# A two-layer decoder trunk on one core: other banks for one score span, and two changes of order on the engines

## Chip, core and metric

The kernel runs on one core of one Trainium2 chip. The metric is the device time of one execution in microseconds (us), given as the median of several runs; lower is better. A core has several engines that work side by side, each through a stream of instructions of its own: TensorE (PE) multiplies matrices and writes its results into eight PSUM banks, ScalarE (ACT) and VectorE (DVE) work on the elements of tiles, GpSimd (POOL) does a few small things here, and SyncE (SP) issues most of the transfers from memory.

## What is computed

The input is 512 tokens of 1024 numbers. Each of the two layers is a mixer and then a feed-forward network (FFN), each with a root-mean-square norm ahead of it and behind it and a residual sum. Cut to what matters here:

```python
for i in range(2):
    h = even_mixer(rms_norm(x, pre_g)) if i == 0 else odd_mixer(rms_norm(x, pre_g))
    x = x + rms_norm(h, post_g)
    h = conv_ffn(rms_norm(x, ffn_pre_g[i]), ...)      # (silu(gate) * up) @ w_down
    x = x + rms_norm(h, ffn_post_g[i])

def stick_breaking_attention(q, k, v):                # part of odd_mixer
    z = q @ k.T * scale
    log_beta = log_sigmoid(z)
    log_keep = where(strict, log_sigmoid(-z), 0)
    after = cumsum(log_keep, reverse=True) - log_keep
    return where(strict, exp(log_beta + after), 0) @ v
```

## The kernel before, in words

**Stages.** The program goes once through first mixer, first FFN, second mixer, second FFN, for all 512 tokens. Tokens are cut into four tiles of 128, taken in the order 3, 2, 1, 0 (`ORDER`). Every fp32 product is made from three products of halves (`mm3`, L263 to L265): each operand is split into a high part (ACT copies it, L72 or L171) and a low part (DVE subtracts, L73 or L172).

**Columns.** The next stage needs the normed tokens as columns. For a tile i, `mean_square` squares and sums X[i] on ACT (L188) and POOL makes the factor (L178, L181); `normed` multiplies on DVE in two halves (L546 in the first FFN, L1284 in the second mixer); `turned` gives back a function that, when called, transposes eight blocks on PE (L211) into two banks and splits each bank into xh (ACT, L171) and xl (DVE, L172). "Columns" below means this function.

**Sums.** `part_of` multiplies half of a tile's output by the gain on DVE (L225) and squares it on ACT (L230), and the residual is added on DVE (L542, L1308) once POOL has the factor (L180, L181).

**Banks.** The eight banks are rings by tag: "a" has three, "s" two, "t", "o" and "n" one each. A tile that takes a bank waits until the one that last had it has been read.

**Order.** In most stages a scheduler orders each engine's stream. At the end of the first FFN (from L530) and at the second mixer's end (from L1289) a `manual_schedule` keeps PE, DVE, ACT and POOL in the order in which the program is written; only the splits of weights are put in between. Weights come by DMA into three raw buffers, are split ahead of time into five pairs of buffers, and a pair is free again when PE has used it.

**Place 1: stick-breaking scores** (`sb_scores`, from L1047). For each of two pairs of heads, scores stand in three spans of 512, 384 and 384 columns; the third holds two blocks, of 256 and 128 columns. Each span takes two banks, one for each head y, and the two heads' products use two halves of PE's rows. PE makes the scores (L1057), DVE adds the mask to each block (L1061), and later instructions make the weights; in between PE makes four projections (`proj_T`, banks of ring "a", tile apt). Spans 1 and 3 both take the two banks of ring "s".

**Place 2: the second mixer's end** (loop from L1290). For each tile n: 12 products into the first half's bank, then the square of the tile before (X[j]), then the first half's product and square, then the columns of the tile before that one (`turns.pop(0)()`), then 12 products of the second half. The last two tiles' columns are called from inside the second FFN's first products (at k of 2 and 6), which read tiles 3 and 2 first (tile u, L263 to L265).

**Place 3: the first FFN's last sum** (from L553). `bank_done("c", 1)` makes the last 12 products (4 terms of 3) into a bank that `part_of` reads afterwards; columns of tile 3 stand ahead of it. The products of the second mixer (tile av) follow.

Of the kernel before, what the change touches and what calls it, by code (L numbers as in the profile page):

```python
# [86 lines left out]
def trunk(tc, A, out):  # L87
# [3 lines left out]
    with ExitStack() as top:  # L91
# [15 lines left out]
        def bank(tag, name, *shape):  # L107

            t = pp.tile([P, S], F32, tag=tag, name=name, bufs=BANKS[tag])
            if not shape:  # L110
                return t[:]
            n = math.prod(shape)
            names = "abc"[:len(shape)]
            return t[:, :n].rearrange(f"p ({' '.join(names)}) -> p {' '.join(names)}",
                                      **dict(zip(names, shape)))
# [89 lines left out]
        def turned(i, xnT, tags, xn):  # L205

            def turn():
                for n, k0 in enumerate((0, 4)):
                    tp = bank(tags[n], "tp", 4, P)
                    for k in range(4):  # L210
                        PE.transpose(tp[:, k], xn[:, (k0 + k) * P:(k0 + k + 1) * P], ident[:])  # L211
                    d = (slice(None), slice(k0, k0 + 4), slice(i * P, (i + 1) * P))
                    split(xnT[0][d], xnT[1][d], tp)

            return turn

        def part_of(t, ms, n, a, g, between=None, dve_first=False):

            c = slice(n * S, n * S + S)
            o = t[:, c]  # L220
            if isinstance(a, tuple):
                DVE.tensor_tensor(o, *a, ALU.subtract)  # L222
                a = o
            def product():
                DVE.tensor_tensor(o, a, g[:, c], ALU.mult)  # L225

            if dve_first:
                product()
            junk = chp.tile([P, D], BF16, tag="junk", name="junk", bufs=1)
            ACT.activation(junk[:, :S], a, AF.Square, scale=D ** -0.5, accum_out=ms[:, n:n + 1])  # L230
            if between:
                between()
            if not dve_first:
                product()

        def begin(pool=None, tag="s"):
            return ((pool or chp).tile([P, D], F32, tag=tag, name="t", **({"bufs": 2} if tag in ("z", "sp") else {})),
                    begin_sum())
# [22 lines left out]
        def mm3(o, lh, ll, rh, rl, first, last, more=False):  # L261

            PE.matmul(o, lh, rh, start=first, stop=False, skip_group_check=more)  # L263
            PE.matmul(o, lh, rl, start=False, stop=False, skip_group_check=more)  # L264
            PE.matmul(o, ll, rh, start=False, stop=last, skip_group_check=more)  # L265
# [17 lines left out]
        def row_product(acc, terms, first, last, halves=(0, 1)):  # L283

            for half in halves:
                c = slice(half * S, half * S + S)
                for n, (lh, ll, wh, wl) in enumerate(terms):
                    mm3(acc[half], lh, ll, wh[:, c], wl[:, c], first and n == 0, last and n == len(terms) - 1)
# [57 lines left out]
        def ffn(layer, xnT, pending, final):  # L346
            with ExitStack() as es:
# [15 lines left out]
                for half in (1, 0):  # L363
                    t = slice(half * 2 * P, (half + 1) * 2 * P)
# [32 lines left out]
                for n, f in enumerate(PAIRED):  # L397
# [4 lines left out]
                    for z in range(2):  # L402
# [8 lines left out]
                        c = cw[:, f, z]  # L411
# [33 lines left out]
                def product(m, s, g, at, w, half, first, last, more=False):  # L445
                    t = slice(at * P, (at + 1) * P)
                    c = slice(half * S, half * S + S)
                    mm3(bk[m, s], g[0][:, t], g[1][:, t], w[0][:, c], w[1][:, c], first, last, more)
# [34 lines left out]
                def later_product(m, s, n, ws):  # L483
                    at, w, half = PLAN[m]
                    product(m, s, later[n], at(s), ws[w], half, False, n == HF - 1, True)
# [24 lines left out]
                ws = [[W.next(), W.next()] for _ in range(TAIL)]  # L510
                nx = None if final else new_xnT()

                def bank_done(m, s):
                    for n in range(TAIL):
                        later_product(m, s, HF - TAIL + n, ws[n])
                    return bk[m, s]

                if final:

                    with tc.manual_schedule(engines={DVE.engine, ACT.engine, POOL.engine}):  # L520
                        for s in range(2):
                            i, j = 3 - 2 * s, 2 - 2 * s
                            t, ms = begin()
# [20 lines left out]
                def normed(i, r, t):  # L544
                    for c in (slice(0, S), slice(S, D)):
                        DVE.scalar_tensor_tensor(t[:, c], X[i][:, c], r[:, 0:1], g_next[:, c], ALU.mult, ALU.mult)  # L546

                def turn(i, t):
                    return turned(i, nx, "tn", t)

                (t2q, m2), (t0, m0) = early_q
                t3, m3 = begin()
# [14 lines left out]
                q2 = mean_square(X[2][:])  # L567
                b1 = bank_done("b", 1)
                DVE.tensor_tensor(t1[:, S:], uu[:, 1], b1, ALU.subtract)
                turn(3, t3)()  # L570
                part_of(t1, m1, 1, t1[:, S:], g_post, lambda: normed(2, q2, t2q))
                r1 = rstd(m1[:, 0:1], m1[:, 1:2])
                c1 = bank_done("c", 1)
                W.ahead(W.pos + 4)
                add_to(1, t1, r1)
                q1 = []
# [1 line left out]
                def last():  # L578
# [5 lines left out]
                turns = [(4, turn(2, t2q), lambda: (q1.append(mean_square(X[1][:])), last())),  # L584
                         (5, turn(1, t1), lambda: q1.append(mean_square(X[0][:]))),
                         (6, lambda: normed(0, q1[1], t0), turn(0, t0))]
# [370 lines left out]
        def odd(xnT, pending, order):  # L957
            xh, xl = xnT
            with ExitStack() as es:
# [56 lines left out]
                for i in ORDER:  # L1016
                    t = slice(i * P, (i + 1) * P)
                    a = bank("a", "av12")
                    at, *parts = pending.pop(0) if pending else (KD, )
                    for k in range(KD):  # L1020
# [4 lines left out]
                        c = slice((k % 2) * 512, (k % 2 + 1) * 512)  # L1025
# [23 lines left out]
                def sb_scores(u):  # L1049

                    zs = [sb.tile([P, 1280], F32, tag="z", name="z", bufs=2) for _ in range(2)]
                    for n, (j0, o0, o1) in enumerate(spans):
                        zp = [bank(t, "zp") for t in ("ss", "nt", "ss")[n]]
                        for j in (j0,) if j0 < 2 else (2, 3):
                            for y in range(2):
                                r = slice(y * 64, y * 64 + 64)
                                PE.matmul(zp[y][:, off[j] - o0:off[j + 1] - o0], sk[u][r, j * P:(j + 1) * P],  # L1057
                                          sq[u][r, j * P:], start=True, stop=True)
                        for y in range(2):
                            for j in (j0,) if j0 < 2 else (2, 3):  # L1060
                                DVE.tensor_tensor(zs[y][:, off[j]:off[j + 1]], zp[y][:, off[j] - o0:off[j + 1] - o0],  # L1061
                                                  smask[:, :S - j * P], ALU.add)

                    sps = []
                    for z in zs:
                        sp = sb.tile([P, 1280], F32, tag="sp", name="sp", bufs=2)
                        DVE.tensor_scalar(sp[:], z[:], 40.0, None, ALU.min)
                        ACT.activation(sp[:], sp[:], AF.Exp)
                        sps.append(sp)
                    return list(zip(zs, sps))  # L1070
# [217 lines left out]
                norms, turns = [], []  # L1288
                with tc.manual_schedule(engines={PE.engine, DVE.engine, ACT.engine, POOL.engine}):  # L1289
                    for n, i in enumerate(ORDER):  # L1290
                        q = slice(i * P, (i + 1) * P)
                        acc = [bank("as"[i % 2], "ao") for _ in range(2)]
                        terms = [(oS[0][:, k, q], oS[1][:, k, q], *wout[2 + k]) for k in range(2)]
                        terms += [(oG[0][k][:, q], oG[1][k][:, q], *wout[k]) for k in range(2)]
                        t, ms = begin(sb, ("z", "sp")[n % 2])
                        row_product(acc, terms, True, True, (0,))
                        if n:
                            j, tj = norms.pop()
                            rj = mean_square(X[j][:])
                        part_of(t, ms, 0, acc[0], g_post, dve_first=True)  # L1300
                        if n > 1:
                            turns.pop(0)()
                        row_product(acc, terms, True, True, (1,))
                        if n:
                            normed(j, rj, tj)
                        part_of(t, ms, 1, acc[1], g_post)
                        r = rstd(ms[:, 0:1], ms[:, 1:2])
                        DVE.scalar_tensor_tensor(X[i][:], t[:], r[:, 0:1], X[i][:], ALU.mult, ALU.add)  # L1308
                        norms.append((i, t))
                        turns.append(turned(i, nx, "na", t))  # L1310

                    r = mean_square(X[i][:])
# [6 lines left out]

        xnT = even()  # L1320
        xnT = ffn(0, *xnT, False)
        xnT = odd(*xnT)
        ffn(1, *xnT, True)


# [97 lines left out]
```

## Time and profile before

| | us |
|---|---|
| median of 3 runs (1162.73 to 1166.18) | 1164.73 |
| the profiled execution's own time | 1163.55 |
| its span, first to last instruction | 1161.8 |
| PE busy in it | 1143.3 |
| DVE busy | 810.8 |
| ACT busy | 557.9 |

A page of the profile describes one execution. PE's multiplications are pipelined, so the row of one lasts longer than the distance to the next: the distance of two starts says what one costs. In a timeline, a row gives start, duration, engine, line, operation, tiles (out<-in), shape and count, and in brackets the idle time ahead of it and what ended it.

### The profile page before, as it was taken

To read this page: it belongs to the slowest core of one execution; us is meant where nothing else is said; L and a number is where in the kernel's file an instruction comes from. 1 tells how busy PE (TensorE), PEld (TensorE's weight loads), DVE (VectorE), ACT (ScalarE), POOL (GpSimd) and SP (SyncE) were. 2 spreads that over 40 slices of the span, in tenths; PEclk is the share of its full clock that TensorE was granted. 3 is DMA by queue.
4 is the path that set the end of the run, shared out by engine and by line. 5 is a ranking of instruction groups with operands and counts; after the bars stand their busy time and mean duration, and the time that the engine had idled before them with its cause. 6 is when DMAs were issued, how large, how long until landed. Compare 5 with 4: busy or idle time off the path is not lost. (4 is left out here: it accounts for less than half of the span.)

```text
span 1161.8 us, 15175 instructions
## 1 busy us (share of the span) xinstructions
PE 1143.3 (98%) x5656; PEld 940.0 (81%) x5656; DVE 810.8 (70%) x1424; ACT 557.9 (48%) x942; POOL 57.0 (5%) x138
## 2 busy tenths in 40 slices
PE   8999999999999999999999999999999999999997
PEld 7876667898888888888888877898988888888885
DVE  6677676467766766899874465577676666679895
ACT  5565555245434434456543454545443443445562
POOL 2100012110000000000030000002000000000001
PEclk9999999999999999999999999999999999999999
DMA  7310521034333332355826213222233333324461
GB/s 278 121 64 1 170 73 37 37 130 128 93 104 93 94 105 84 100 156 162 251 93 177 73 55 93 92 73 94 91 109 96 104 91 97 103 82 145 145 200 73
DMA packets 39049, 126.81 MB, mean 109 GB/s; under 512 B 4672, under 2 KB 6336, under 8 KB 38848
## 3 DMA queue, kind: packets, MB, share of 16 engines
q1 hardware_dynamic: 37056, 122.11, 33.5%
q10 hardware_dynamic: 1920, 3.74, 1.1%
q8 instruction: 44, 0.72, 0.3%
q14 instruction: 29, 0.24, 0.1%
HBM read 117.95 MB, written 6.29 MB: 107 GB/s over the span
## 5 line engine op out<-in xcount | busy, mean ns | idle before, releaser
L73 DVE TENSOR_TENSOR wl<-wraw,wh 128x1024 fp32r<-128x1024 f32 (+1 forms) x202 | 244.4, 1218 | 181.1 <-ACT wh L72 180.9
L72 ACT CAST wh<-wraw 128x1024 fp32r<-128x1024 f32 (+1 forms) x202 | 209.5, 1046 | 282.8 <-PE u L264 179.4
L263 PE MATMUL u<-xh,wh 128*128 128x512 f32 (+1 forms) x768 | 285.0, 372 | 0.9 <-ACT xh L171 0.9
L264 PE MATMUL u<-xl,wh 128*128 128x512 f32 (+1 forms) x768 | 285.2, 372 | 0.1
L265 PE MATMUL u<-xh,wl 128*128 128x512 f32 (+1 forms) x768 | 285.1, 371 | 0.0
L263 PEld LDWEIGHTS u<-xh,wh 128*128 128x128 f32 x768 | 144.5, 188 | 26.3 <-ACT xh L171 1.3
L264 PEld LDWEIGHTS u<-xl,wh 128*128 128x128 f32 x768 | 144.7, 188 | 25.1 <-DVE xl L172 0.3
L265 PEld LDWEIGHTS u<-xh,wl 128*128 128x128 f32 x768 | 144.7, 188 | 24.8
L265 PE MATMUL acc<-wh,gl 128*128 128x512 f32 x248 | 96.5, 389 | 0.0
L264 PE MATMUL acc<-wl,gh 128*128 128x512 f32 x248 | 96.5, 389 | 0.0
L263 PE MATMUL acc<-wh,gh 128*128 128x512 f32 x248 | 96.4, 390 | 0.0
L417 ACT ACTIVATE y<-y 128x512 f32<-128x512 f32 x44 | 27.7, 632 | 85.1 <-DVE y L415 85.1
L412 ACT ACTIVATE y<-u,cw 128x512 f32<-128x512 f32 x88 | 67.4, 773 | 1.7 <-PE u L265 1.7
L415 DVE SCALAR_TENSOR_TENSOR y<-u,cw,y 128x510 f32<-128x510 f32 x88 | 65.6, 747 | 2.5
L413 DVE SCALAR_TENSOR_TENSOR y<-u,cw,y 128x511 f32<-128x511 f32 x88 | 65.1, 743 | 0.9 <-ACT y L412 0.9
L178 POOL TENSOR_TENSOR rv<-ms,epst 128x1 f32<-128x1 f32 x40 | 10.5, 263 | 913.7 <-ACT junk L230 841.4
L263 PEld LDWEIGHTS acc<-wh,gh 128*128 128x128 f32 x248 | 46.6, 188 | 10.2 <-issue 0.6
L265 PEld LDWEIGHTS acc<-wh,gl 128*128 128x128 f32 x248 | 46.6, 188 | 9.8
L264 PEld LDWEIGHTS acc<-wl,gh 128*128 128x128 f32 x248 | 46.6, 188 | 9.5
L263 PE MATMUL apt<-xh,wh 128*128 128x512 f32 x128 | 50.6, 395 | 0.0
L264 PE MATMUL apt<-xl,wh 128*128 128x512 f32 x128 | 50.0, 391 | 0.0
L265 PE MATMUL apt<-xh,wl 128*128 128x512 f32 x128 | 49.9, 390 | 0.0
(298 smaller groups left out, 1905.7 us busy)
## 6 DMA issues: line engine op xcount, KB each, us to landing
wraw<-in_ffn_w_up SPq DMA_DIRECT2D x88, 512.0 KB, 3.6
wraw<-in_ffn_w_down SPq DMA_DIRECT2D x44, 512.0 KB, 3.7
wraw<-in_od_w_dqk SPq DMA_DIRECT2D x12, 512.0 KB, 3.7
wraw<-in_ffn_w_down SPq DMA_DIRECT2D x22, 256.0 KB, 2.7
wraw<-in_ev_w_dqk SPq DMA_DIRECT2D x8, 512.0 KB, 4.0
wraw<-in_ev_w_out SPq DMA_DIRECT2D x8, 512.0 KB, 3.6
spill<-X SPq DMA_DIRECT2D x8, 512.0 KB, 2.6
X<-spill SPq DMA_DIRECT2D x8, 512.0 KB, 6.3
```

What stands on the lines that cost most here:

```text
L72: self.nc.scalar.copy(h[:, :w], raw[:, :w])
L73: self.nc.vector.tensor_tensor(l[:, :w], raw[:, :w], h[:, :w].bitcast(F32), ALU.subtract)
L178: POOL.tensor_tensor(v[:, :n], ms, epst[:, :n], ALU.add)
L263: PE.matmul(o, lh, rh, start=first, stop=False, skip_group_check=more)
L264: PE.matmul(o, lh, rl, start=False, stop=False, skip_group_check=more)
L265: PE.matmul(o, ll, rh, start=False, stop=last, skip_group_check=more)
L412: ACT.activation(y[:, z], u, AF.Identity, bias=c[:, 3:4], scale=c[:, 2:3])
L413: DVE.scalar_tensor_tensor(y[:, z, 1:], u[:, :S - 1], c[:, 1:2], y[:, z, 1:], ALU.mult, ALU.add)
L415: DVE.scalar_tensor_tensor(y[:, z, 2:], u[:, :S - 2], c[:, 0:1], y[:, z, 2:], ALU.mult, ALU.add)
L417: ACT.activation(y[:, 0], y[:, 0], AF.Silu)
```

## The change

Three edits, each in one place.

```diff
-                def bank_done(m, s):
+                def bank_done(m, s, between=None):
                     for n in range(TAIL):
                         later_product(m, s, HF - TAIL + n, ws[n])
+                        if between and n == 1:
+                            between()
                     return bk[m, s]
...
                 DVE.tensor_tensor(t1[:, S:], uu[:, 1], b1, ALU.subtract)
-                turn(3, t3)()
+                c1 = bank_done("c", 1, turn(3, t3))
                 part_of(t1, m1, 1, t1[:, S:], g_post, lambda: normed(2, q2, t2q))
                 r1 = rstd(m1[:, 0:1], m1[:, 1:2])
-                c1 = bank_done("c", 1)
...
-                        zp = [bank(t, "zp") for t in ("ss", "nt", "ss")[n]]
+                        zp = [bank(t, "zp") for t in ("ss", "nt", "aa")[n]]
...
                         row_product(acc, terms, True, True, (0,))
+                        if n > 1:
+                            turns.pop(0)()
                         if n:
                             j, tj = norms.pop()
                             rj = mean_square(X[j][:])
                         part_of(t, ms, 0, acc[0], g_post, dve_first=True)
-                        if n > 1:
-                            turns.pop(0)()
                         row_product(acc, terms, True, True, (1,))
```

In the built streams the edits move the following. PE, first FFN: six of the last twelve products stand ahead of tile 3's eight transposes. PE, scores: the third span's four products go head by head in turn (256, 256, 128, 128) where they went one head after the other (256, 128, 256, 128), and they no longer wait for DVE's additions. PE, second mixer's end: nothing; at the second FFN's start the first products stand in the order L263, L264, L265, bank by bank, where four of L263 stood first. ACT, second mixer's end: the two copies to xh stand ahead of the square of X[j], for two tiles, and one weight copy stands one square earlier. DVE there: the two splits to xl stand ahead of the first half's product, and the last two weight splits stand one between and one behind the two halves of tile 1's `normed`. POOL and SP issue the same in the same order.

## Prediction

> **What bounds the kernel now.** I read the page first: its parts 1 and 2 give busy time and granted clock, part 5 the costliest groups (here the splits of weights on DVE, 1218 ns each).
>
> ```profile
> span 1161.8 us, 15175 instructions
> PE 1143.3 (98%) x5656; PEld 940.0 (81%) x5656; DVE 810.8 (70%) x1424; ACT 557.9 (48%) x942; POOL 57.0 (5%) x138
> ...
> PEclk9999999999999999999999999999999999999999
> ...
> L73 DVE TENSOR_TENSOR wl<-wraw,wh 128x1024 fp32r<-128x1024 f32 (+1 forms) x202 | 244.4, 1218 | 181.1 <-ACT wh L72 180.9
> ```
>
> PE is busy for 98% of the span at a granted clock of 0.9 or more of full speed in every slice. Work on the other engines costs time only where PE waits for it, and at most 1161.8 - 1143.3 = 18.5 us of idle PE is there to be taken. Next the waits of PE: who waited, for whom, us in total, times, longest.
>
> ```profile
> PE zp L1057 <- DVE z L1061: 1.1, 2, 0.8
> PE u L263 <- ACT xh L171: 0.9, 1, 0.9
> PE tp L211 <- DVE t L546: 0.3, 1, 0.3
> ```
>
> The three rows are the three places of the change, and together 2.3 us. But an idle row counts only time in which no product was still in flight, and the modelled ends of products run on into a wait. So I price each place by distances between starts on PE's timeline, and what could be late next by DVE's, ACT's and POOL's.
>
> The Trainium skill says the same in "Perfetto Trace Analysis", section Identifying the Most-Contended Engine: busy time of pipelined products is no measure of what is left on TensorE. By idle rows the change would be worth 2.3 us at most; by starts, as the trace bears out below, more than twice that.
>
> **Place 3, the first FFN's last sum.** PE's timeline there:
>
> ```profile
> 586.29 0.39 PE L264 MATMUL acc<-wl,gh 128*128 128x512 f32 x1
> 586.52 0.39 PE L265 MATMUL acc<-wh,gl 128*128 128x512 f32 x1
> ...
> 587.24 1.32 PE L211 MATMUL tp<-ident,t 128*128 128x128 f32 x8 [0.33 <-DVE t L546]
> 588.31 0.48 PE L263 MATMUL acc<-gh 128*128 128x512 f32 x1
> ...
> 591.13 0.39 PE L263 MATMUL av<-wh,xh 128*128 128x512 f32 x1
> ...
> 593.86 1.03 PE L211 MATMUL tp<-ident,t 128*128 128x128 f32 x8
> 594.65 0.48 PE L263 MATMUL av<-wh,xh 128*128 128x512 f32 x1
> ```
>
> Products start 586.52 - 586.29 = 0.23 us apart, so PE could have gone on at 586.75. The transposes of tile 3 start at 587.24 and the next product at 588.31, 1.07 us later; undisturbed, at 593.86, the same eight take 594.65 - 593.86 = 0.79. What they waited for is on DVE:
>
> ```profile
> 586.43 1.41 DVE L546 SCALAR_TENSOR_TENSOR t<-X,rr,gain 128x512 f32<-128x512 f32 x2 [0.71 <-POOL rr L181]
> 588.95 1.28 DVE L172 TENSOR_TENSOR xl<-tp,xh 128x512 fp32r<-128x512 f32 x2
> ```
>
> `normed` of tile 3 (L546, two halves in 1.41 us) ends at 587.84; its second half is late for the second four blocks too. Loss: (588.31 - 586.75) - 0.79 = 0.77 us. With six products ahead the transposes start at 586.75 + 6 x 0.23 = 588.1, behind 587.84, so all 0.77 us goes. What is late next: xl of tile 3. Its first bank is filled about 0.6 us after the transposes' start, ACT's copy of it (0.6) ends near 589.4, and DVE's two splits (1.28 us) run from there to 590.7. The mixer's first product now starts at 591.13 and then at 590.36; the third one, L265 with xl, at 590.8, with the first split done at 590.1. The cover is 0.7 us; what goes beyond it is paid. I take -0.75; bounds -0.3 (the idle row) to -0.77.
>
> **Place 1, the scores.** The rows of the first pair of heads, then of the second (narrow stretches, since a wide one merges rows):
>
> ```profile
> 648.93 0.70 PE L1057 MATMUL zp<-sq,sk 64*128 64x512 f32 x2
> ...
> 649.89 0.49 PE L1057 MATMUL zp<-sq,sk 64*128 64x384 f32 x2
> 650.22 0.49 PE L1057 MATMUL zp<-sq,sk 64*128 64x384 f32 x2
> 650.84 0.48 PE L1057 MATMUL zp<-sq,sk 64*128 64x256 f32 x1
> ...
> 652.57 0.92 PE L1057 MATMUL zp<-sq,sk 64*128 64x256 f32 x4 [0.82 <-DVE z L1061]
> 653.42 0.50 PE L263 MATMUL apt<-xh,wh 128*128 128x512 f32 x1
> ...
> 669.87 0.39 PE L1088 MATMUL cp<-sh,tri 128*128 128x512 f32 x1
> ...
> 683.45 1.77 PE L1057 MATMUL zp<-sq,sk 64*128 64x512 f32 x8
> 685.53 1.51 PE L1057 MATMUL zp<-sq,sk 64*128 64x256 f32 x8 [0.30 <-DVE z L1061]
> 686.98 0.50 PE L263 MATMUL apt<-xh,wh 128*128 128x512 f32 x1
> ```
>
> Each product has two rows, for two passes. Two heads' passes run beside each other: two of 384 columns start at 649.89, the next two at 650.22, so a pair of passes takes 0.33, and one could have started at 650.55. In the third span the first head starts at 650.84, alone, the second at 652.57, and the first projection at 653.42. Side by side, two pairs of passes of 256 and two of 128 columns take, by 0.33 per 384, 2 x 0.22 + 2 x 0.11 = 0.66 us; with 0.1 for the change of shape the projection starts at 651.3. Gain 653.42 - 651.3 = 2.1 us. Second pair of heads: eight rows from 683.45, by the same pattern (1.62 us to the next free start, as from 648.93 to 650.55) free at 685.07; the projection then starts at 685.83 instead of 686.98: 1.15 us. If the two heads did not run side by side, each span would take 1.3 us instead of 0.66 and the gain would be 2.1 - 0.65 and 1.15 - 0.65, or 1.95 in all.
>
> The Trainium skill, "TensorEngine Tiling (Array Packing)", section Key Properties, says that row tiles run in parallel, and its Gotcha 1 that they must not write one bank at a time. Here each head has its own bank, and the two rows of 384 columns within one 0.49 us agree: by the rule 3.25 us, without it 1.95.
>
> What is late next. Ring "a": the two banks were read long before by the value tiles' copies, and the next projection takes the third bank. The second projection needs the first head's bank again, after DVE's additions:
>
> ```profile
> 651.83 2.67 DVE L1061 TENSOR_TENSOR z<-zp,smask 128x512 f32<-128x512 f32 x7
> ...
> 666.75 1.48 DVE L172 TENSOR_TENSOR sl<-sp,sh 128x1280 fp32r<-128x1280 f32 x1
> ```
>
> They end at 651.83 + 2.67 = 654.5 (DVE runs through without waiting for PE, so they come no earlier); the second projection starts a projection after 651.3. Three projections take 669.87 - 653.42 = 16.45, one 5.5, so it starts at 656.8, 2.3 us later. Then the products with tri (L1088, at 669.87) need sl, split at 666.75 for 1.48 us, ending 668.2. PE would be there at 667.75, too early by 0.45 if DVE stood still; but ahead of sl stands ACT's copy of the first projection's result, which comes with PE, so I let this chain move about 1.4 us and count nothing. If not, 0.45 us is lost. I take -3.2; bounds -1.1 (the idle row) to -3.3.
>
> **Place 2, the second mixer's end.** PE, then ACT, POOL and DVE:
>
> ```profile
> 800.98 1.03 PE L211 MATMUL tp<-ident,t 128*128 128x128 f32 x8
> ...
> 804.36 0.39 PE L265 MATMUL ao<-wo,og 128*128 128x512 f32 x1
> 805.67 0.74 PE L263 MATMUL u<-xh,wh 128*128 128x256 f32 x4 [0.93 <-ACT xh L171]
> ...
> 808.97 1.04 PE L211 MATMUL tp<-ident,t 128*128 128x128 f32 x8
> ...
> 815.59 1.04 PE L211 MATMUL tp<-ident,t 128*128 128x128 f32 x8
> ```
>
> ```profile
> 802.47 1.06 ACT L188 ACTIVATE junk<-X 128x1024 bf16<-128x1024 f32 x1 [3.27 <-DVE X L1308]
> 805.05 1.06 ACT L171 CAST xh<-tp 128x512 fp32r<-128x512 f32 x2
> 809.61 1.07 ACT L171 CAST xh<-tp 128x512 fp32r<-128x512 f32 x2 [1.98 <-PE tp L211]
> ...
> 822.29 1.05 ACT L72 CAST wh<-wraw 128x1024 fp32r<-128x1024 f32 x1 [4.99 <-PE u L264]
> ```
>
> ```profile
> 803.97 0.55 POOL L181 TENSOR_TENSOR rr<-rv,mhalf 128x1 f32<-128x1 f32 x1
> ```
>
> ```profile
> 805.73 1.28 DVE L172 TENSOR_TENSOR xl<-tp,xh 128x512 fp32r<-128x512 f32 x2
> 806.93 1.40 DVE L1284 SCALAR_TENSOR_TENSOR t<-X,rr,gain 128x512 f32<-128x512 f32 x2
> ```
>
> Products end at 804.36 + 0.23 = 804.59, and the second FFN starts at 805.67, when ACT has made xh of tile 2. The transposes of tile 2 had started at 800.98; elsewhere ACT copies 809.61 - 808.97 = 0.64 us after their start, here 4.07 after it, since square and weight copy (from 802.47) stood ahead. Then the stretch up to the next transposes (24 products) takes 808.97 - 805.67 = 3.30, where 48 products later take 815.59 - 808.97 - 0.79 = 5.83, so 24 take 2.9: another 0.4 lost, waiting for xl (805.73). With columns ahead: xh from 801.62 to 802.7, xl (1.28 us) to 803.5, both before 804.59. PE goes on at 804.59 and reaches the transposes of tile 1 at 807.55 instead of 808.97: 1.42 us.
>
> What is late next is a ring: copy, square of the next tile, factor, `normed`, transposes. From the transposes' start: 0.64 to the copy, 0.96 for two copies, 1.16 for the square (1.06, and 0.1 of readout, to 803.63), 0.9 for POOL (its last step ends at 803.97 + 0.55 = 804.52), 1.40 for `normed` (L1284): 5.06. PE has 24 products and transposes, 24 x 0.23 + 0.79 = 6.3 us, in the loop, and 807.55 - 800.98 = 6.57 for tile 1. Of the two weight splits that now stand at `normed` of tile 1, one (1.2 us, the page's L73) is inside: 6.26, against 6.57 plus 0.4, since its second half is needed only by the fifth block. So nothing is late, by 0.7 to 1.2 us. For tile 0 DVE's part comes about 1.2 us earlier, by the 1.28 us of xl (805.73) that no longer stand ahead of `normed`, and PE by 1.42; the cover there I put at 0.5, an estimate. SP: the split just ahead of 805.73 frees a raw buffer, and now ends near 806.5; the weights loaded there are copied by ACT at 822.29, so 15 us cover it. I take -1.4; bounds -0.9 (the idle row) to -1.5.
>
> **Sum.** -0.75 - 3.2 - 1.4 = -5.35 us, rounded to -5.4; bounds -2.3 to -5.6; none reaches above nothing, since no edit adds work to PE, and a loss needs the third rival's chain. PE does the same products, and behind each place it waits for nothing that the list of its waits shows, so what it gains it keeps. Against the profiled execution's own 1163.55: 1158.2. The median of three, 1164.73, lies 1.2 above that one; a median is what will be given again, so I forecast 1164.73 - 5.4 = **1159.3**.
>
> **The rivals.**
> 1. *Half of it* (18%). Only the idle rows go: PE comes early and waits for the next thing, sl behind the scores and `normed` at the mixer's end. For it: covers of 0.4 to 0.7 us are thin. Against it: the chains that feed them move along. 1164.73 - 2.3 = 1162.4; with half the rest, 1160.9.
> 2. *Given back* (11%). A stage with a pace of its own, such as transfers, takes up all of it: 1164.7. Against: no transfer is among PE's waits.
> 3. *Slower* (5%). At the mixer's end the ring becomes one chain: if ACT's and DVE's parts stand behind each other instead of side by side, it has also xl 1.28, two products with the gain 0.68 each, one split 1.2 and the residual 1.28: 5.06 + 5.1 = 10.2 us a tile against PE's 6.4, 3.8 late for each of three tiles: 11.4 - 5.4 = 6 slower, 1170.7. It decides from 6.4 + 5.4/3 = 8.2 us a tile. Against: DVE's list has xl ready to run while ACT squares.
>
> **How the numbers follow.** The forecast has 66%. A measurement of this kernel can tell about 0.3%, 3.5 us, so faster begins at 1161.2. Faster: 64 of the forecast's 66 and 6 of the first rival's 18, together 70%. Within 0.3%: 2 + 12 + 11 = 25%. Slower: 5%. The range reaches from the whole bound taken from a median as low as the lowest run (1162.73 - 5.6, rounded to 1157.0) to the first rival (1162.4), rounded to 1162.6; it leaves out the other two rivals.
>
> **What would show it.** Right: no wait of PE for z at L1057, and the first projection 2.4 us or less after the first score row instead of 4.5; PE's transposes of tile 3 in 0.8 us with no idle time ahead; the second FFN's first product less than 0.4 us after the last one of the mixer, and 6.6 us between the transposes of tiles 2 and 1. Wrong: a new wait of PE for sl at L1088, for `normed` at L211, or for xl at L264, or PE stretches that grow behind the three places by what these lost.

## The result, and the profile after

| | median of 5 runs, us | lowest to highest |
|---|---|---|
| before | 1164.13 | 1162.73 to 1166.18 |
| changed | 1157.79 | 1157.08 to 1158.78 |

The ratio is 0.9944, with a 95% interval of 0.9933 to 0.9955: the change makes the kernel 6.3 us (0.56%) faster, and the interval allows 5.2 to 7.8 us. The forecast was 1159.3 us, with a gain of 5.4.

The page of the changed kernel, its span, its line for PE and its granted clock in 40 slices:

```profile
span 1157.0 us, 15177 instructions
...
PE 1140.5 (99%) x5656; PEld 939.4 (81%) x5656; DVE 810.9 (70%) x1424; ACT 557.2 (48%) x942; POOL 58.4 (5%) x138
...
PEclk9999999999999999999999999999999999999999
```

The span fell by 4.8 us, PE's idle time only from 18.5 to 1157.0 - 1140.5 = 16.5 us, by 2.0: the rest was hidden in the modelled ends of rows, as the prediction warned. The whole list of PE's waits (who waited, for whom, us in total, times, longest):

```profile
PE ac L263 <- ACT xh L171: 2.2, 1, 2.2
PE tpp L622 <- DVE s L858: 1.5, 1, 1.5
PE sps L845 <- DVE st L611: 1.2, 2, 0.8
PE warm L137 <- DVE zero L134: 1.1, 1, 1.1
PE tp L211 <- DVE xn L201: 0.8, 2, 0.6
PE tpp L622 <- DVE odl L172: 0.6, 1, 0.6
PE o L870 <- DVE otok L872: 0.4, 2, 0.2
PE tc L687 <- DVE ctok L681: 0.2, 1, 0.2
```

The three rows of before (zp for z, u for xh, tp for t) are gone, and none for sl, for `normed` in the second mixer or for xl has come. Line numbers behind the first edit are one or two higher than in before.

**Place 3.** PE, then DVE:

```profile
588.47 0.40 PE L265 MATMUL acc<-gh,gl 128*128 128x512 f32 x1
588.71 1.03 PE L211 MATMUL tp<-ident,t 128*128 128x128 f32 x8
589.50 0.47 PE L263 MATMUL acc<-gh 128*128 128x512 f32 x1
...
590.27 0.40 PE L263 MATMUL acc<-gh 128*128 128x512 f32 x1
```

```profile
587.02 1.42 DVE L548 SCALAR_TENSOR_TENSOR t<-X,rr,gain 128x512 f32<-128x512 f32 x2 [0.71 <-POOL rr L181]
...
589.96 1.29 DVE L172 TENSOR_TENSOR xl<-tp,xh 128x512 fp32r<-128x512 f32 x2 [0.33 <-ACT xh L171]
```

`normed` ends at 588.44, the transposes start at 588.71, one product's distance (0.24) behind the start of the last product, and the eight take 589.50 - 588.71 = 0.79 us instead of 1.07. The first half of xl is done by 590.6 (half of the 1.29 us from 589.96), and its product, the third of the mixer, starts at 591.43.

**Place 1.** First pair of heads, second pair, and the two sides of the sl chain:

```profile
648.89 2.43 PE L1058 MATMUL zp<-sq,sk 64*128 64x512 f32 x16
651.24 0.50 PE L263 MATMUL apt<-xh,wh 128*128 128x512 f32 x1
...
667.72 0.39 PE L1089 MATMUL cp<-sh,tri 128*128 128x512 f32 x1
...
681.27 2.43 PE L1058 MATMUL zp<-sq,sk 64*128 64x512 f32 x16
683.63 0.50 PE L263 MATMUL apt<-xh,wh 128*128 128x512 f32 x1
```

```profile
665.11 1.48 DVE L172 TENSOR_TENSOR sl<-sp,sh 128x1280 fp32r<-128x1280 f32 x1
```

All sixteen rows of a pair now merge into one, as nothing interrupts them. The first projection comes 2.35 us after the first score, where it came 653.42 - 648.93 = 4.49 us after it; the second pair's comes 2.36 us after, instead of 3.53. Counted from the first score, the split of sl starts 665.11 - 648.89 = 16.22 us after it instead of 17.82, so it came 1.60 us earlier; it ends at 666.59, 1.1 us ahead of the products that need it.

**Place 2.** PE, ACT and DVE:

```profile
797.72 1.03 PE L211 MATMUL tp<-ident,t 128*128 128x128 f32 x8
...
801.11 0.39 PE L265 MATMUL ao<-wo,og 128*128 128x512 f32 x1
801.33 0.28 PE L263 MATMUL u<-xh,wh 128*128 128x256 f32 x1
...
804.20 1.04 PE L211 MATMUL tp<-ident,t 128*128 128x128 f32 x8
```

```profile
798.36 1.07 ACT L171 CAST xh<-tp 128x512 fp32r<-128x512 f32 x2 [2.33 <-PE tp L211]
799.32 1.07 ACT L188 ACTIVATE junk<-X 128x1024 bf16<-128x1024 f32 x1
```

```profile
801.41 0.75 DVE L1285 SCALAR_TENSOR_TENSOR t<-X,rr,gain 128x512 f32<-128x512 f32 x1 [0.55 <-POOL rr L181]
802.08 1.22 DVE L73 TENSOR_TENSOR wl<-wraw,wh 128x1024 fp32r<-128x1024 f32 x1
803.22 0.75 DVE L1285 SCALAR_TENSOR_TENSOR t<-X,rr,gain 128x512 f32<-128x512 f32 x1
```

The copy to xh follows the transposes by 0.64 us, the second FFN starts 0.22 us behind the mixer's last product, and the transposes of tiles 2 and 1 are 804.20 - 797.72 = 6.48 us apart instead of 7.99.

### The profile page after: what moved, and what is told of

It is laid out like the page before. It is cut to its first block, busy times and chain, and to the rows that moved or that the text cites. A ratio compares the mean times of both kernels' runs of the same rounds, so it can differ in the third digit from the quotient of the medians.

```text
span 1157.0 us, 15177 instructions
## 1 busy us (share of the span) xinstructions
PE 1140.5 (99%) x5656; PEld 939.4 (81%) x5656; DVE 810.9 (70%) x1424; ACT 557.2 (48%) x942; POOL 58.4 (5%) x138
## 5 line engine op out<-in xcount | busy, mean ns | idle before, releaser
L72 ACT CAST wh<-wraw 128x1024 fp32r<-128x1024 f32 (+1 forms) x202 | 209.4, 1046 | 280.8 <-PE u L264 179.5
L263 PE MATMUL u<-xh,wh 128*128 128x512 f32 (+1 forms) x768 | 285.4, 372 | 0.0
L264 PE MATMUL u<-xl,wh 128*128 128x512 f32 (+1 forms) x768 | 285.3, 371 | 0.0
L265 PE MATMUL u<-xh,wl 128*128 128x512 f32 (+1 forms) x768 | 285.2, 371 | 0.0
L263 PEld LDWEIGHTS u<-xh,wh 128*128 128x128 f32 x768 | 144.7, 188 | 25.0
L265 PEld LDWEIGHTS u<-xh,wl 128*128 128x128 f32 x768 | 144.7, 188 | 24.9
L264 PEld LDWEIGHTS u<-xl,wh 128*128 128x128 f32 x768 | 144.7, 188 | 24.9
L264 PE MATMUL acc<-wl,gh 128*128 128x512 f32 x248 | 96.5, 389 | 0.0
L265 PE MATMUL acc<-wh,gl 128*128 128x512 f32 x248 | 96.5, 389 | 0.0
L263 PE MATMUL acc<-wh,gh 128*128 128x512 f32 x248 | 96.4, 390 | 0.0
L417 ACT ACTIVATE y<-y 128x512 f32<-128x512 f32 x44 | 27.7, 632 | 85.0 <-DVE y L415 84.9
L263 PEld LDWEIGHTS acc<-wh,gh 128*128 128x128 f32 x248 | 46.6, 188 | 10.2 <-issue 0.5
L265 PEld LDWEIGHTS acc<-wh,gl 128*128 128x128 f32 x248 | 46.6, 188 | 9.6
L264 PEld LDWEIGHTS acc<-wl,gh 128*128 128x128 f32 x248 | 46.6, 188 | 9.6
L263 PE MATMUL apt<-xh,wh 128*128 128x512 f32 x128 | 50.6, 396 | 0.0
L264 PE MATMUL apt<-xl,wh 128*128 128x512 f32 x128 | 50.0, 391 | 0.0
L265 PE MATMUL apt<-xh,wl 128*128 128x512 f32 x128 | 49.9, 390 | 0.0
```

The costliest lines, as they stand in the source:

```text
L72: self.nc.scalar.copy(h[:, :w], raw[:, :w])
L417: ACT.activation(y[:, 0], y[:, 0], AF.Silu)
```

## Experiments

Every kernel has the same 5656 products on PE (one has ten more). So each run can be laid beside before product by product, and a stage is the distance from the start of one product to that of a later one. This is sharper than the whole time: the stretch up to 30 us varies from 27.7 to 29.8 us between executions, and the first mixer from 229.3 to 231.1, whatever the kernel. The table has the lengths of five stages in us (place 3; first pair of heads; second pair; tiles 2 to 1 and tiles 1 to 0 at the mixer's end), and the time (median where there are several runs). The stages are cut so wide that whatever an edit moves stays inside one: in before they can be read from 584.25 to 593.40, 645.00 to 660.12, 682.06 to 690.06, 800.06 to 812.11 and 812.11 to 823.05.

| kernel | place 3 | pair 1 | pair 2 | 2 to 1 | 1 to 0 | time (runs) |
|---|---|---|---|---|---|---|
| before | 9.15 | 15.12 | 8.00 | 12.05 | 10.94 | 1163.55 (this execution) |
| changed | 8.41 | 13.01 | 6.87 | 10.53 | 10.94 | 1157.79 (5) |
| all_three | 8.37 | 13.01 | 6.87 | 10.53 | 10.94 | 1158.62 (5) |
| scores_alone | 9.15 | 13.01 | 6.87 | 12.06 | 10.94 | 1159.61 (5) |
| columns_alone | 9.15 | 16.70 | 8.04 | 10.58 | 10.94 | 1162.20 (11) |
| ffn_alone | 8.37 | 15.16 | 8.04 | 12.07 | 10.94 | 1162.89 (11) |
| heads_in_turn_off | 9.26 | 13.09 | 6.93 | 12.07 | 10.94 | 1159.89 (1) |
| last_columns_only | 9.17 | 16.74 | 8.00 | 10.53 | 10.94 | 1163.30 (1) |
| longer_ring | 9.15 | 16.74 | 8.04 | 12.47 | 11.99 | 1167.78 (1) |
| columns_after_all | 9.17 | 15.12 | 8.04 | 12.07 | 10.94 | 1164.51 (1) |
| before_again_1 | 9.17 | 15.12 | 8.04 | 12.02 | 10.94 | 1163.50 (1) |
| before_again_2 | 9.16 | 15.12 | 8.00 | 12.05 | 10.94 | 1164.59 (1) |

The theory was that of the prediction: three losses that do not touch each other, each given back whole. The rivals were its first two: only the idle rows go, or the gain is given back later.

**Each place alone, and all together.** Before with one edit of the change each, and with all three. Before ran 21 times beside them, 1164.07 us in the median (1162.79 to 1166.88).

```diff
+                        zp = [bank(t, "zp") for t in ("ss", "nt", "aa")[n]]
```

> Place 1 alone. Theory (price by starts, gains independent): PE's starts fall 2.0 to 2.1 us back behind the first pair of heads and 1.15 behind the second, 3.2 us in all, and stay there; time 3.2 us below the kernel before. Rival (only idle rows count): 1.1 us. Rival (the three places hold each other up, so one alone gives little): under 1 us.

Measured: ratio 0.9964 (0.9952 to 0.9977), 4.5 us by the medians (the interval allows 2.7 to 5.6); by stages 2.11 and 1.13, together 3.24.

```diff
+                        if n > 1:
+                            turns.pop(0)()
                         if n:
                             j, tj = norms.pop()
...
-                        if n > 1:
-                            turns.pop(0)()
```

> Place 2 alone. Theory: 1.45 us at the second FFN's start (1.08 of distance to its first product and 0.4 in its first 24 products), kept to the end. Rival (idle rows): 0.9 us. Rival (ring of columns, square and normed becomes the pace): no gain or slower, with a wait of PE at the transposes of tile 1 or 0.

Measured: ratio 0.9981 (0.9972 to 0.9990), 1.9 us; by its stage 1.47. In the profiled execution the first pair of heads, which this kernel does not touch, took 16.70 us instead of 15.12; more of that below.

```diff
+                c1 = bank_done("c", 1, turn(3, t3))
...
-                turn(3, t3)()
```

> Place 3 alone. Theory: 0.77 us at the transposes of tile 3, kept. Rival (idle row): 0.3 us. Rival (xl of tile 3 late for the mixer's third product): gain taken back at the first product with xl, near 0. A time alone can't tell these apart (under 0.1%); PE's starts can.

Measured: ratio 0.9992 (0.9983 to 1.0001), 1.2 us; by its stage 0.78. By the time alone this one is not told from nothing; by its stage it is.

> The three edits together, as in the changed kernel. Theory: 0.77 + 3.2 + 1.45 = 5.4 us, the sum of the three alone. Rival (something beyond the three places moved too, as the changed kernel's 6.3 us against 5.4 could mean): over 6 us, with PE's starts changing at a fourth place.

Measured: ratio 0.9950 (0.9938 to 0.9963), 5.5 us; by stages 0.78 + 2.11 + 1.13 + 1.52 = 5.54, and single edits 0.78 + 3.24 + 1.47 = 5.49. The three add up, and no later stage gives anything back: the stages that the table leaves out agree within 0.1 us, but for the first two, which vary, and the FFNs, where single executions, of before too, are up to 0.8 us longer. Both rivals fall.

**Does the order of the heads matter?** The banks of the change, with the third span's products one head after the other in the stream (256, 128 of one head, then 256, 128 of the other). In before this is the order of the first pair only: its built stream takes the second pair's heads in turn already (256, 256, 128, 128), as the changed kernel does for both, so what is said of this order under "The change" holds for the first pair alone.

```diff
+                        zp = [bank(t, "zp") for t in ("ss", "nt", "aa")[n]]
-                        for j in (j0,) if j0 < 2 else (2, 3):
-                            for y in range(2):
-                                r = slice(y * 64, y * 64 + 64)
+                        for y in range(2):
+                            r = slice(y * 64, y * 64 + 64)
+                            for j in (j0,) if j0 < 2 else (2, 3):
```

> Place 1 alone, but in the third span each head's two products stand one after the other (256, 128, then 256, 128). Theory (two heads' passes run beside each other only when they stand in turn): 0.6 to 0.65 us less gain at each pair of heads, so PE's starts fall back by 1.4 and 0.5 us, 1.95 in all. Rival (side by side is no matter, only the wait for DVE went): 3.2 us as before.

Its PE, and a narrow stretch of the same (649.92 to 649.93):

```profile
648.12 2.53 PE L1057 MATMUL zp<-sq,sk 64*128 64x512 f32 x16
650.58 0.50 PE L263 MATMUL apt<-xh,wh 128*128 128x512 f32 x1
```

```profile
649.73 0.48 PE L1057 MATMUL zp<-sq,sk 64*128 64x256 f32 x2
```

The projection comes 2.46 us after the first score instead of 2.35 as in the changed kernel, and the stages lose 0.08 and 0.06 us, not 0.65 each. Two products on two halves of the rows overlap in either order, as soon as none of them waits: both heads' products of 256 columns start at 649.73, although the first head's product of 128 columns stands between them in the built stream. Why they need not start in the order of the stream, the run does not show. What kept the heads apart in before was the wait itself: the second pair lost 1.13 us there with its heads in turn.

**Which tile's columns bring the gain of place 2?** Columns ahead of the square only in the last round (tile 2's).

```diff
+                        if n == 3:
+                            turns.pop(0)()
...
+                        if n > 1 and not (n == 3):
                             turns.pop(0)()
```

> Place 2 for the last tile of the loop alone (tile 2's columns ahead of the square of X1), tile 3's columns as before. Theory (only tile 2's columns are late for the second FFN): the whole 1.45 us. Rival (the two rounds share the gain): about half.

The stage is 10.53 us, the whole gain of 1.5 with one of two moves. Tile 3's columns need not have moved: nobody waits for them. (The time of this run shows less, since pair 1 took 16.74 us in it; that is the subject of the last experiment.)

**Is the ring at the mixer's end real?** Place 2 alone, with two more squares of X[j] (results unused) in each of the two rounds.

```diff
+                            for _ in range(2 if n > 1 else 0):
+                                junk, more = ...
+                                ACT.activation(junk[:], X[j][:], AF.Square, scale=D ** -0.5, accum_out=more[:])
```

> Place 2 alone, with two more squares of X on ACT between columns and square for the last two tiles (added work of 2 x 1.0 us in the ring each round; their results are not used). Theory (a ring with 0.6 to 1.3 us of cover): PE still gains at the second FFN's first product, but waits at transposes: tile 2 about 0.7 us late (5.06 + 2.0 against 6.3), tile 1 another 1 us; net place 2 gives between 0 and 1 us slower than before. Rival (the squares lie off PE's path): 1.45 us of gain stay.

The waits of PE in that kernel, the row that is new; then ACT between the transposes of tiles 2 and 1:

```profile
PE tp L211 <- DVE t L1284: 2.2, 3, 0.9
```

```profile
804.73 1.19 ACT L171 CAST xh<-tp 128x512 fp32r<-128x512 f32 x2 [1.05 <-PE tp L211]
806.03 1.05 ACT L72 CAST wh<-wraw 128x1024 fp32r<-128x1024 f32 x1
806.99 1.05 ACT L1303 ACTIVATE junk<-X 128x1024 bf16<-128x1024 f32 x1
...
808.04 1.03 ACT L72 CAST wh<-wraw 128x1024 fp32r<-128x1024 f32 x1
808.98 1.05 ACT L1303 ACTIVATE junk<-X 128x1024 bf16<-128x1024 f32 x1
...
810.22 1.06 ACT L188 ACTIVATE junk<-X 128x1024 bf16<-128x1024 f32 x1
```

The two stages grow by 1.9 and 1.05 us over place 2 alone, and PE now waits for `normed` before the transposes of tiles 2, 1 and 0. So the third rival's chain exists, and a longer one does cost: together 12.47 + 11.99 is 1.5 us more than before, where 0 to 1 was expected. Two things differ from what was meant: two weight copies (L72, 0.96 and 0.94 us from start to start) came to stand ahead of the last square, and 12 more products stand ahead of tile 1's transposes. The run therefore shows the ring, and not the exact cover.

**How thin is the cover at place 3?** Place 3 alone, with all twelve products ahead of the transposes instead of six (the edit is shown against the changed kernel).

```diff
-                        if between and n == 1:
+                        if between and n == 3:
```

> Place 3 alone, with all twelve products ahead of tile 3's columns. Theory (cover of 0.7 us for xl, used up by six more products of 0.23): transposes without wait, but the mixer's first products wait 0.6 us or so for xh and xl of tile 3, so 0.1 to 0.2 us of gain is left. Rival (columns are covered further): 0.77 us stay.

```profile
590.11 0.39 PE L265 MATMUL acc<-gh,gl 128*128 128x512 f32 x1
590.34 1.03 PE L211 MATMUL tp<-ident,t 128*128 128x128 f32 x8
591.61 0.50 PE L263 MATMUL av<-wh,xh 128*128 128x512 f32 x1 [0.24 <-ACT xh L171]
...
592.34 0.50 PE L265 MATMUL av<-wh,xl 128*128 128x512 f32 x1
592.67 0.39 PE L263 MATMUL av<-wh,xh 128*128 128x512 f32 x1
```

The transposes follow the products without a gap, and yet the whole gain is gone (9.17 us against 9.15 in before), where 0.1 to 0.2 us of it was expected to stay. From the start of the transposes to the fourth product behind them it takes 592.67 - 590.34 = 2.33 us, in the changed kernel 590.27 - 588.71 = 1.56: the first product waits for xh, the third (L265) for xl, and 0.77 us is lost. So six products behind the transposes (6 x 0.23 = 1.4 us) hide copy and split, and without them 0.77 us is paid: 0.6 us of what they hide is spare, against the 0.7 of the prediction. The run also shows that a stall can move whole to the other side of the transposes.

**What is the long pair of heads in columns_alone?** In three of the eight profiles with the old banks the stage of the first pair takes 16.7 us instead of 15.1. Two views of columns_alone, first the stretches (length, then busy us of PE, PEld, DVE, ACT, POOL, each with its count; then granted clock, DMA share, GB/s), then PE:

```profile
648.00:652.00 4.00, 3.05 (x17) 1.77 (x13) 3.81 (x7) 2.10 (x2) 0.00 (x0) 0.99 0.50 144
652.00:656.00 4.00, 4.00 (x11) 3.21 (x12) 2.43 (x6) 2.27 (x2) 0.00 (x0) 0.59 0.36 122
656.00:660.00 4.00, 4.00 (x20) 3.30 (x19) 0.00 (x0) 0.93 (x3) 0.00 (x0) 1.00 0.00 0
```

```profile
647.39 2.82 PE L1057 MATMUL zp<-sq,sk 64*128 64x512 f32 x12
651.03 0.92 PE L1057 MATMUL zp<-sq,sk 64*128 64x256 f32 x4 [0.82 <-DVE z L1061]
651.88 0.80 PE L263 MATMUL apt<-xh,wh 128*128 128x512 f32 x1
...
652.89 0.63 PE L265 MATMUL apt<-xh,wl 128*128 128x512 f32 x1
653.32 0.63 PE L263 MATMUL apt<-xh,wh 128*128 128x512 f32 x1
```

One of these stretches in before, of which the prediction quotes rows of PE:

```profile
652.00:656.00 4.00, 3.43 (x15) 2.83 (x16) 3.97 (x9) 0.73 (x1) 0.00 (x0) 1.00 0.65 208
```

Right behind the scores the granted clock is 0.59 for 4 us, and products start 653.32 - 652.89 = 0.43 us apart instead of 0.23. The trace's records of the clock change in steps of 3.41 us, and one step, from 651.9, has 0.5. A theory of its own: the slow stage of scores itself (4.49 us, with products on 64 of 128 rows and the wait in it) makes the clock drop afterwards; the rival: the drop is chance. If the theory holds, filling the wait with work keeps the clock up, and before without a change shows the drop now and then. Three runs test it: before with 7 and 3 unused products in the waits of the two pairs (their bank is read by nobody; the first pair's heads now go in turn in the built stream), and before itself twice.

```diff
+                        if n == 2:
+                            idle = bank("a", "idle")
+                            for _ in range(3 if u else 7):
+                                PE.matmul(idle, xh[:, 0, :P], xh[:, 0], start=True, stop=True)
```

> The kernel before (banks of ring s, so the wait for DVE stays), with products whose result is not used put into the wait: seven of 128x512 ahead of the first pair's third span, three ahead of the second's. Theory (a granted clock of one half for 3.41 us behind the scores comes when PE was little used through a stretch of the scores): the scores take 4.5 us as before, no stretch of half clock follows them, no execution has a mean clock of 0.995 or less (6 of 21 of the kernel before have), the median is 0.3 to 0.6 us below the kernel before. Rival (the half clock comes from elsewhere): one or two of five at 0.995 or less.

> The kernel before, unchanged, for its trace. Theory: with a chance of 3 to 5 in 10 a stretch of 3.41 us at half clock starts 1.5 to 4.9 us behind the first score row and costs 1.6 us there, when one of the clock's 3.41 us windows begins 0 to 2 us behind the first score row; otherwise none. Rival: half clock with no such relation.

> The kernel before, unchanged, a second time. Theory: a stretch of 3.41 us at half clock behind the first pair's scores with a chance of 3 to 5 in 10, when a 3.41 us window of the clock begins 0 to 2 us behind the first score row. Rival: half clock with no such relation.

The PE of wait_filled:

```profile
649.10 1.77 PE L1061 MATMUL zp<-sq,sk 64*128 64x512 f32 x8
650.80 1.91 PE L1056 MATMUL idle<-xh 128*128 128x512 f32 x7
652.64 1.01 PE L1061 MATMUL zp<-sq,sk 64*128 64x256 f32 x8
653.59 0.50 PE L263 MATMUL apt<-xh,wh 128*128 128x512 f32 x1
```

The products fill the wait and cost nothing (4.49 us from the first score to the projection, as in before). The clock behind the scores stayed at 1.0. The mean granted clock of its 11 runs lies between 0.996 and 0.998, but this decides nothing: columns_alone, with the wait unfilled, has none at 0.995 or less among its 11 runs either. The median did not fall as expected: 1164.11 us, ratio 1.0005 (0.9996 to 1.0014) against 1163.49 us of before in 15 runs beside it. Neither of the two profiles of before shows the drop. So the drop is real, and what brings it on is only in part settled; what the profiles say for it stands in the last section.

## Why the prediction was right, point by point

**What bounds the kernel** was right: PE sets the end, and each wait that went is kept to the last instruction. That idle rows count too little was right as well: 2.3 us by the rows, 5.5 measured by starts. What the page's row of clock digits could not show was missed: a slice is 1161.8 / 40 = 29 us, so 3.4 us at half clock leave 0.94 of full speed, and the digit is still a 9. Before's own trace has such a stretch in its first slice: 0.50 from 13.08 to 16.49, and 0.94 for the slice.

**Place 3** (-0.75): measured 0.74 and 0.78. The cover of 0.7 us for xl was 591.43 - 590.6 = 0.8 by the rows of the changed kernel, and 0.6 by what columns_after_all lost.

**Place 1** (-3.2): 2.11 + 1.13 by stages, against 2.1 + 1.15. The sl chain moved by 1.60 us, where 1.4 was taken, and ends 1.1 us early; nothing new is late. The prediction priced the case "If the two heads did not run side by side" at 0.65 us a span, and the expectation of heads_in_turn_off tied it to the order in the stream. That reason failed: the order is worth 0.14 us for both spans together, and the heads ran one after the other in before because the second head's products waited. So the 0.65 belonged to the wait from the start, and the sum was right because the wait went. That row tiles run in parallel, the rule that the prediction takes from the Trainium skill ("TensorEngine Tiling (Array Packing)", Key Properties), agrees with the runs in both orders.

**Place 2** (-1.4): 1.47 and 1.52. The forecast was a little low by its own figures: 24 products take 5.83 / 2 = 2.92 us and from 804.59 reach 807.51, not 807.55, which makes 1.46. The ring came out as written: from the transposes at 797.72 by 5.06 and one split of 1.2 us `normed` should end at 803.98, and it ends at 803.97. PE's part is 6.48 us, not 6.57, so the cover of tile 1's second half is 804.20 + 0.4 - 803.97 = 0.63, just under the stated 0.7 to 1.2. Tile 0 (stage 1 to 0, 10.94 us in both) lost nothing. The third rival's mechanism is there, as longer_ring shows; its price was not reached since in the changed order a tile needs 803.97 - 797.72 = 6.25 us of ring, not the 8.2 from which it decides.

**The sum** of 5.35 became 0.74 + 2.11 + 1.13 + 1.52 = 5.50 in the profiled execution of the changed kernel, and 5.54 in all_three. The time, 1157.79, is 1.5 us below the forecast. 0.6 of it is the start: 1164.73 was the median of three runs, five gave 1164.13 and 21 others 1164.07. The other 0.9 is a gain of 6.3 for 5.4. Both are inside the interval (5.2 to 7.8), and all_three, the same order of work measured again, gave 5.5. Part may be the half clock, which no term of the sum had: of the 21 runs of before beside all_three, 6 have a mean granted clock of 0.995 or less, and average 1165.56 us, where the other 15 average 1163.72; none of 15 runs of the changed banks has so low a clock. That would be worth 6 / 21 x 1.8 = 0.5 us on average; of the 15 later runs of before only 2 are so low, which makes it half of that. It is argued, not shown, and weakly: the mean does not tell where in the execution the half clock lies. In 11 of the 13 profiles a step of it starts between 10 and 14 us, all have one at the end, and columns_alone, whose profile has the drop behind the scores, has a mean of 0.997. And wait_filled should have gained the same and did not. Where the 0.9 comes from stays open.

## What to carry to other kernels

Where a pipelined engine is the bound, price a stall by the distance of starts on both sides of it against the same stretch elsewhere undisturbed, not by its idle row: here 2.1, 1.15, 1.4 and 0.75 us were forecast in this way and 2.11, 1.13, 1.5 and 0.74 to 0.78 measured, where the idle rows gave 2.3 us in all, less than half. Then walk the next chain that becomes late, and count what covers it: six products behind eight transposes made the difference between all of 0.75 us and nothing. An order inside one engine's stream may matter only because something in it waits, so ask which it is before a price is put on the order.

## What the runs showed of the hardware

**The clock fell to half behind a stage in which PE was hardly ever idle.** In columns_alone, last_columns_only and longer_ring, one clock record of 3.41 us has 0.5, directly behind the first pair's scores, and pair 1 takes 1.6 us more. PE's longest idle row in that stage is 0.82 us; most of the rest is products on 64 of 128 rows. All changes of the clock in one trace lie whole steps of 3.41 us apart, so the bounds of the steps between them can be counted. What sets these three apart from the five other profiles with the old banks is where these bounds fall: the step ahead of the drop began 1.1, 1.7 and 1.6 us after the first score, so that it held the wait and little else than scores (it ended 4.5, 5.1 and 5.0 us after the first score, where the projections start at 4.49); without a drop (before, ffn_alone, columns_after_all and the two repeats) one began 2.0 to 2.4 us after, or in one case 3.1. In the four profiles with the changed banks, where the stage takes 2.35 to 2.46 us without a wait, less than one step, there was no drop, nor in the one with the wait filled. Three of these five are a fair comparison, since their steps fell much as in the profiles with the drop: one began 1.05 us after the first score in scores_alone, 1.2 in wait_filled and 1.3 in all_three. This fits a rule by which the use of PE in one such window sets the clock of the next; 13 profiles are consistent with it, and no run placed a window on purpose. The Trainium skill, "TensorE: Matmul & The Clock Gate", Part 1, describes such free-running windows of about 3.4 us and a clock of half or full, and the 0.5 and the 3.41 us agree; its table of the two states lets the clock drop after an idle window, where the window here had less than 1 us of idle row.

**Unused products in a wait cost nothing**: in wait_filled seven full-width products left the first pair's distance from score to projection at 4.49 us, and three the second pair's at 3.52, as the engine would have stood still.

**Products on different halves of the rows need not start in the order of the stream**: in heads_in_turn_off both heads' products of 256 columns start at 649.73, with one of 128 columns between them in the built stream.
